# Wider query and output projections, paired modulations, shared visits for the linear attention's products and another job order in a two-layer hybrid block

## The chip, the cores and the metric

The kernel runs on one core of one Trainium2 chip. The metric is the device time in microseconds of one execution. The engines are TensorE (PE in the profile, with PEld for its weight loads), VectorE (DVE), ScalarE (ACT), GpSimd (POOL) and SyncE (SP), which here only issues DMAs.

## What is computed

Two layers of a block with three branches over 512 latent tokens (x) and 256 context tokens (c), 1024 channels, fp32 inputs. Cut to what matters here:

```python
def hybrid_layer(xs, cs, c, c_ctx, ..., need_ctx):
    shift_x, scale_x, gate_x = jnp.split(jax.nn.silu(c) @ w_mod + b_mod, 3, axis=-1)
    ...
    hx = rms_norm(xs, norm_g) * (1 + scale_x[:, None]) + shift_x[:, None]
    px = split_cols(hx @ w_in + b_in)
    ya_x = conv_module(*px[0:3], dw_w, dw_b, ln_g, ln_b, w_conv_out)      # 31 taps
    yb_x, yb_c = gla_branch(px[3:9], pc[3:9], ...)                        # both directions
    yc_x, yc_c = attn_branch(px[9:13], pc[9:13], ...)                     # softmax attention
    def merge(p, ya, yb, yc):
        return (jax.nn.sigmoid(p[13]) * ya + jax.nn.sigmoid(p[14]) * yb
                + jax.nn.sigmoid(p[15]) * yc) @ w_out
    xs = xs + gate_x[:, None] * merge(px, ya_x, yb_x, yc_x)
```

The context is updated in layer 0 only. The linear attention (`gla_branch`) has 4 heads and chunks of 64 tokens, 12 over both streams: in each chunk a state S = diag(decay) S + k^T v is carried on, in both directions, and the output is a masked product within the chunk plus q S.

## The kernel before

Every large product is made of two-part fp32r numbers: weights and activations are split in a high and a low part (`whi`, `wlo`; two tiles of `hx` for x, of `hc` for the context), and a sum over 1024 channels is 8 x 3 = 24 matrix products: high by high, low by high, high by low.

An order planner in the kernel (`Weaver`, with costs in `Engine` and the table `P`) runs the work as coroutines when the program is built, takes the ready one with the lowest priority number on each engine, and so fixes the order in which each engine's instructions stand. A recording helper makes them all, so that line 296 stands at nearly every row of the profile; groups are told apart by their tiles. The two strings `P["o0"]` and `P["o1"]` list each layer's jobs, which PE works through in turn: `q` query, key and value projections, `c` convolution inputs, `v` and `k` inputs of the linear attention, `s` and `m` gates of branches and merge, `a`, `g`, `h` modulations, and two digits for a merge job (branch, column block). Attention, linear attention, convolution and norms are further coroutines whose instructions are woven in between.

PSUM's eight banks are three pairs of tiles: `pg` and `pm`, one bank each, and `p2` (`p` in the rows), two banks each. A coroutine asks for them with `need` and gives them back with `free`. SBUF has 29 big buffers (`r3`, `r` in the rows).

The parts that the change touches:
- `TM` (line 608): a projection with tokens on the output partitions. It waits for two weight units of 4 x 256 columns, and for each token tile of 128 makes 24 products of 256 columns into one `pg` bank. `attn_jobs` (line 910) has three such jobs: keys and values for six tiles, and two halves of the query for the tiles of `qtt` (six in layer 0, four in layer 1).
- `Mod` (line 628): a column block of the modulation, with 32-column products (`r,cstat` in the rows, two records each). `mod_jobs` makes eight jobs a layer, each followed by a copy, two transposes, a reduction and six small DVE instructions; `gate_jobs` four.
- `gla_head` (line 1452): after six transposes, `states` makes the chunks' products in two blocks (8, then 6), each in one `p2` tile, and DVE carries the states on with 12 and 10 instructions of 64 x 128; `intra` makes the masked products, four to a `p2` tile, and DVE copies them under the mask (`zt`). Two heads are under way at a time.
- `OutJob` (line 1777): the output projection in four blocks of 256 columns for x and c of layer 0 and x of layer 1. It first broadcasts a piece of the gate row (`yg`) over the partitions by one product, waits for all eight pieces of the merged sum (`M`), and for each token tile makes 24 products of 256 columns into a `pg` bank; `out_ev` multiplies by the gate (`tg<-pg,gb`) and adds to the residual (`r<-r,tg`).

Of the kernel before, what the change touches and what calls it, by code (L numbers as in the profile page):

```python
# [43 lines left out]
def _consts():  # L44
# [4 lines left out]
    for v in range(2):  # L49
        for g in range(4):  # L50
# [25 lines left out]
P = dict(vb=3, pko=5, res=4, resg=0, lead=6, pbr=3, tlead=3, nf=2, nbk=4, pconv=7, mlead=2, pmain=8, lat=6,  # L76
         vm=100, am=100, gm=97)
P["o0"] = (
# [3 lines left out]
P["o1"] = (  # L82
    "c3 q0 m22 q1 q2 c0 m11 m15 c1 c6 h3 m4 m8 s11 c2 s3 s10 s5 k0 m7 s9 s2 m12 s4 s8 c5 c4 m19 c7 v1 h2 m14 "
    "v0 k1 m9 m20 k2 m16 m0 h1 s7 m21 m18 k3 m5 m23 s6 s0 s1 m17 h0 m2 m3 m10 21 22 20 23 m1 m6 m13 00 03 02 "
    "10 11 01 13 12")
# [20 lines left out]
class Weaver:  # L106
# [18 lines left out]
    def pool(self, tag, cap):  # L125
        self.avail[tag] = [0.0] * cap
# [174 lines left out]
def hybrid_kernel(ctx: ExitStack, tc: tile.TileContext, x, c, ctx_in, c_ctx, norm_g, w_mod, b_mod,  # L301
# [57 lines left out]
    gbt = mk(pr, "gb", 2)  # L359
# [4 lines left out]
    W.pool("rm", 12)  # L364
# [262 lines left out]

    class Mod:
        def __init__(self, L, cols, evac, step=4):
            self.L, self.cols, self.evac, self.step = L, cols, evac, step  # L630
            self.evs = [_Event() for _ in range(2 * len(cols))]
            self.raws = []

        def load(self):
            src = w_mod[self.L.l].rearrange("(p j) c -> p j c", j=8)
            for i in range(2 * len(self.cols)):
                yield from need(("rm", 1))
                yield from W.need_low(1)
                r = r3([4, 128])
                self.raws.append(r)  # L640
                c0 = self.cols[i // 2]
                spawn(load(self.evs[i], (r, src[:, i % 2 * 4:i % 2 * 4 + 4, c0:c0 + 128])), 0)

        def run(self):
            yield from need(("pg", 1))
            ps = pg([len(self.cols) * 128])
            n = 2 * len(self.cols)
            for i0 in range(0, n, self.step):
                yield from wait(*self.evs[i0:i0 + self.step])
                yield "+P"  # L650
                for i in range(i0, min(n, i0 + self.step)):
                    for j in range(4):
                        PE.matmul(ps[32 * j:32 * j + 32, i // 2 * 128:i // 2 * 128 + 128],
                                  lhsT=K["cstat"][:, i % 2 * 4 + j], rhs=self.raws[i][:, j],
                                  start=(i % 2 == 0), stop=(i % 2 == 1), tile_position=(0, 32 * j))
                    free("r3")
                    free("rm")
            spawn(self.evac(ps), 1)

    class Layer:  # L660
# [65 lines left out]
        def mod_jobs(S):  # L726
# [4 lines left out]
            def evac(j):  # L731
                def g(ps):
                    yield from need(("tg", 1))
                    yield "E"
                    yt = tg([256])
# [4 lines left out]
                    pt = pm([2, 128])  # L740
                    for m in range(2):
# [3 lines left out]
                    V.tensor_reduce(S.mc[:, :, j], pt.rearrange("p m (g r) -> p m r g", g=4)[:, :, 0:2, :],  # L745
                                    axis=AX.X, op=ALU.add)
# [4 lines left out]
                    for v, s in enumerate("xc"):  # L751
                        a, b = S.sh[s][:, j:j + 1], S.sc[s][:, j:j + 1]
                        V.tensor_add(a, S.mc[:, 0, j, v:v + 1], vv[:, V_BM + j:V_BM + j + 1])
                        V.scalar_tensor_tensor(b, S.mc[:, 1, j, v:v + 1], 1.0, vv[:, V_BM + 8 + j:V_BM + 9 + j],
                                               op0=ALU.add, op1=ALU.add)
                        V.tensor_mul(b, b, vv[:, V_NG + j:V_NG + j + 1])
                    fire(S.E(("mod", j)))
                return g
            return [Mod(S, [128 * j, D + 128 * j], evac(j), 1 if S.l == 0 and j < 3 else 4) for j in range(8)]

        def gate_jobs(S):
            def evac(u0):
                def g(ps):
# [3 lines left out]
                    cp(S.yg[:, u0 * 256:u0 * 256 + 256], ps)  # L767
                    free("pg")
                    S.ygn += 1
                    if S.ygn == 4:  # L770
# [4 lines left out]
            return [Mod(S, [2048 + u * 256, 2176 + u * 256], evac(u)) for u in range(4)]  # L775
# [134 lines left out]
        def attn_jobs(S):  # L910
            S.qkv = {}
            S.nq = {tt: (3 if tt in S.qtt else 1) for tt in range(6)}

            def mkev(b):
                def ev(tt, ps):
                    yield from wait(S.E("abias"))
                    if tt not in S.qkv:
                        yield from need(("r3", 1))
                        S.qkv[tt] = r3([T])
                    yield "V"  # L920
                    V.tensor_add(S.qkv[tt][:, b * 256:(b + 1) * 256], ps, S.bq[:, b * 256:(b + 1) * 256])
                    free("pg")
# [4 lines left out]
            return [TM(S, [(O_AQ + b * 256, 256)], range(6) if b == 2 else S.qtt, mkev(b)) for b in (2, 0, 1)]  # L927
# [524 lines left out]
        def gla_head(S, h):  # L1452
# [49 lines left out]
            done_s, done_a = _Event(), _Event()  # L1502

            def states():
                step = 0
                for blk, nst in (([0, 1, 2, 3, 11, 10, 4, 5], 6), ([9, 8, 7, 6, 5, 10], 5)):
                    yield from need(("p2", 1))
                    yield "P"
                    pcn = p2([2, 4, 128])
                    cnt = [0, 0]  # L1510
                    con = {}
                    for cix in blk:
                        e = cix % 2
                        r = slice(64 * e, 64 * e + 64)
                        con[cix] = pcn[:, e, cnt[e]]
                        cnt[e] += 1
                        PE.matmul(con[cix], lhsT=kt[r, cix // 2], rhs=gv[h][r, cix // 2], start=True, stop=True)
                    if step == 0:
                        nst = 6
                    for i in range(step, step + nst):  # L1520
                        for o, r in ((fo, F_), (bo, B_)):
                            yield "V" if (i == step and r == F_) else "+V"
                            V.scalar_tensor_tensor(ST(o[i + 1], r), ST(o[i], r), dec[r, o[i]:o[i] + 1], con[o[i]][r],
                                                   op0=ALU.mult, op1=ALU.add)
                    step += nst
                    free("p2")
                free("r3")
                fire(done_s)

            def intra():  # L1530
                step = 2
                for g in range(0, len(S.qtt), step):
                    tts = S.qtt[g:g + step]
                    n = len(tts)
                    yield from need(("p2", 1))
                    yield "+P"
# [189 lines left out]
        def out_ev(S, s, blk, i, ps, gb, dst, lastt):  # L1726
# [6 lines left out]
            if lastt:  # L1733
                free("gb")
# [195 lines left out]
```

## Time and profile before

| | |
|---|---|
| median of 3 runs | 1496.29 us (1494.51 to 1499.57) |
| the profiled execution's own time | 1495.49 us |
| its span in the profile | 1493.7 us |
| PE busy | 1418.5 us, 95% |
| weight loads (PEld) busy | 1239.1 us, 83% |
| DVE busy | 1149.3 us, 77% |
| ACT busy | 582.2 us, 39% |
| DMA | 187.57 MB, 126 GB/s in the mean |

The busy time of an engine is the union of its instructions; the ends of PE's products are modelled, so a busy PE may hold short waits. Tiles in the rows bear the program's names without buffer numbers, and `out<-in` tells what an instruction writes and reads; the moving operand of a product comes first, then the one that stands. A stretch of the span belongs to a stage only roughly, since the stages overlap.

### The profile page before, as it was taken

To read this page: it belongs to the slowest core of one execution; us is meant where nothing else is said; L and a number is where in the kernel's file an instruction comes from. 1 tells how busy PE (TensorE), PEld (TensorE's weight loads), DVE (VectorE), ACT (ScalarE), POOL (GpSimd) and SP (SyncE) were. 2 spreads that over 40 slices of the span, in tenths; PEclk is the share of its full clock that TensorE was granted. 3 is DMA by queue.
4 is the path that set the end of the run, shared out by engine and by line. 5 is a ranking of instruction groups with operands and counts; after the bars stand their busy time and mean duration, and the time that the engine had idled before them with its cause. 6 is when DMAs were issued, how large, how long until landed. Compare 5 with 4: busy or idle time off the path is not lost.

```text
span 1493.7 us, 24919 instructions
## 1 busy us (share of the span) xinstructions
PE 1418.5 (95%) x9520; PEld 1239.1 (83%) x9520; DVE 1149.3 (77%) x2086; ACT 582.2 (39%) x1127; POOL 248.9 (17%) x354
## 2 busy tenths in 40 slices
PE   3999999999999989998999999999999999999998
PEld 2799888888997877776888988977888988777788
DVE  4445977778987988985777574778999899998563
ACT  4423465454225232234423154344545235632320
POOL 2003312120000142100041010502322000121200
PEclk9999999999999999999999999999999999999999
DMA  9732332213232234364667354242122425455752
GB/s 271 206 111 56 93 91 84 63 35 95 80 116 74 62 92 124 104 219 150 199 195 245 112 183 121 78 134 84 50 83 80 123 78 155 117 181 173 250 170 85
DMA packets 235371, 187.57 MB, mean 126 GB/s; under 512 B 15296, under 2 KB 206322, under 8 KB 235252
## 3 DMA queue, kind: packets, MB, share of 16 engines
q1 hardware_dynamic: 234948, 185.86, 40.9%
q8 instruction: 75, 1.23, 0.3%
q14 instruction: 44, 0.36, 0.1%
q10 hardware_dynamic: 304, 0.11, 0.0%
HBM read 151.86 MB, written 34.08 MB: 124 GB/s over the span
## 4 chain that ended last, share of the span: by engine, by line
PE 62%; DVE 21%; issue 5%; POOL 4%; DMA 4%; ACT 3%; SPq 1%; ACTq 0%; DVEq 0%; POOLq 0%
PE pg L296 51%; DVE r L296 12%; PE p L296 6%; PE pm L296 4%; POOL sm L296 4%; DVE wlo L296 4%; DVE sm L296 2%; ACT r L296 1%; DVE tg L296 1%; DMA r<-ogd 1%; DVE t L296 1%; DVE whi L296 1%; SPq L314 1%; DVE zt L296 1%; DMA raw<-in_w_in 1%
## 5 line engine op out<-in xcount | busy, mean ns | idle before, releaser
L296 PE MATMUL pg<-hx,whi 128*128 128x512 f32 x1504 | 384.1, 398 | 1.1 <-ACT tg L296 0.6
L296 PEld LDWEIGHTS pg<-hx,whi 128*128 128x128 f32 x1504 | 275.4, 190 | 56.3 <-ACT tg L296 1.0
L296 DVE SCALAR_TENSOR_TENSOR r<-r,tp,r 128x768 f32<-128x768 f32 (+29 forms) x240 | 202.5, 887 | 0.4
L296 PE MATMUL pg<-hx,wlo 128*128 128x512 f32 x752 | 194.7, 393 | 0.0
L296 DVE TENSOR_TENSOR wlo<-raw,whi 128x1024 fp32r<-128x1024 f32 (+1 forms) x140 | 174.8, 1248 | 20.0 <-ACT whi L296 18.1
L296 ACT CAST whi<-raw 128x512 fp32r<-128x512 f32 (+1 forms) x194 | 115.3, 619 | 191.4 <-PE pg L296 153.6
L296 PE MATMUL pg<-whi,hx 128*128 128x256 f32 (+1 forms) x1152 | 165.4, 285 | 1.8 <-DVE hx L296 0.8
L296 PEld LDWEIGHTS pg<-hx,wlo 128*128 128x128 f32 x752 | 138.9, 188 | 28.2
L296 PEld LDWEIGHTS pg<-whi,hx 128*128 128x128 f32 x1152 | 150.0, 191 | 5.2 <-DVE tg L296 2.9
L296 ACT ACTIVATE tg<-pg,hv 128x256 f32<-128x256 f32 (+1 forms) x116 | 71.7, 618 | 211.5 <-PE pg L296 162.2
L296 DVE TENSOR_TENSOR r<-r,r 128x512 f32<-128x512 f32 (+8 forms) x208 | 123.0, 612 | 23.2 <-DMA r<-ogd 13.5
L296 PE MATMUL pg<-r,whi 128*128 128x512 f32 (+1 forms) x576 | 127.9, 363 | 7.6 <-DVE r L296 7.5
L296 POOL TENSOR_SCALAR r<-r,sm 128x768 f32<-128x768 f32 (+1 forms) x80 | 84.2, 1055 | 272.3 <-DVE sm L296 229.3
L296 PEld LDWEIGHTS pg<-r,whi 128*128 128x128 f32 x576 | 97.1, 190 | 27.1 <-DVE r L296 8.8
L296 PE MATMUL pg<-hc,whi 128*128 128x256 f32 x768 | 108.3, 290 | 4.1 <-DVE r L296 3.2
L296 PEld LDWEIGHTS pg<-hc,whi 128*128 128x128 f32 x768 | 100.6, 195 | 7.8 <-issue 3.6
L296 ACT ACTIVATE r<-p,sm 128x768 f32<-128x768 f32 (+1 forms) x80 | 65.5, 819 | 80.9 <-DVE sm L296 80.7
L296 PE MATMUL pg<-wlo,hx 128*128 128x256 f32 (+1 forms) x576 | 93.4, 284 | 0.0
L296 PE MATMUL p<-r,r 64*128 64x128 f32 (+2 forms) x672 | 90.2, 308 | 2.4 <-DVE r L296 1.1
L296 POOL TENSOR_TENSOR r<-r,r 128x512 f32<-128x512 f32 (+1 forms) x33 | 44.1, 1344 | 281.8 <-DVE r L296 251.1
L296 PE MATMUL pm<-r,r 128*128 128x256 f32 (+4 forms) x672 | 83.1, 283 | 0.9 <-DVE r L296 0.9
L296 PEld LDWEIGHTS pm<-r,r 128*128 128x128 f32 (+2 forms) x672 | 75.6, 176 | 8.4 <-DVE r L296 2.4
(151 smaller groups left out, 2056.9 us busy)
## 6 DMA issues: line engine op xcount, KB each, us to landing
raw<-in_w_in SPq DMA_DIRECT2D x116, 512.0 KB
r<-in_w_mod SPq DMA_DIRECT2D x96, 256.0 KB
thd<-tg SPq DMA_DIRECT2D x48, 256.0 KB
raw<-in_w_out SPq DMA_DIRECT2D x24, 512.0 KB
r<-thd SPq DMA_DIRECT2D x24, 384.0 KB
sgd<-tg SPq DMA_DIRECT2D x24, 256.0 KB
r<-thd SPq DMA_DIRECT2D x24, 256.0 KB
r<-sgd SPq DMA_DIRECT2D x12, 384.0 KB
```

Source lines behind the costliest of these rows:

```text
L296: return real(*a, **k)
L314: (nc.scalar if q else nc.sync).dma_start(dst, src)
```

## The change

- A class `Wide` makes a projection 512 columns wide for all token tiles at once: it takes a bank for each tile, goes through four weight units of 2 x 512 (outer loop) and all tiles (inner loop), and each tile is evacuated after the last unit.
- `QJob` is the query projection in that form (one job for two). In layer 0 its six tiles take both `p2` tiles and both `pg` banks, in layer 1 its four tiles take both `p2` tiles.
- `OutJob` is made in two blocks of 512. It begins when the first two pieces of the merged sum are there and takes the weight units in the order of the merge jobs; the gate row is broadcast before the last unit. The first block of x takes both `p2` tiles, the second both `pg` and both `pm` banks, a block of c one `p2` tile.
- `Mod` jobs are joined in twos (in layer 0: 1, 1, 2, 2, 2 column pairs; in layer 1 four times 2; gates two a layer), with weights loaded in thirds of 3, 3 and 2 rows.
- In `gla_head` one coroutine makes a block of state products and a group of inner products in one visit of PE, and takes a `p2` tile for each at once.
- The job strings and some of the planner's costs and priorities are new.

```diff
-P = dict(vb=3, pko=5, res=4, resg=0, lead=6, pbr=3, tlead=3, nf=2, nbk=4, pconv=7, mlead=2, pmain=8, lat=6,
-         vm=100, am=100, gm=97)
+P = dict(vb=3, pko=12, res=4, resg=0, lead=6, pbr=2, tlead=3, nf=2, nbk=3, pconv=6, mlead=2, pmain=6, lat=6,
+         vm=100, am=100, gm=101)
-    "a3 a2 m19 k3 q2 q1 m2 q0 s11 s4 c3 m5 m3 m9 c4 s3 m22 a4 c1 g0 k1 c0 c2 m0 m16 s1 k0 v0 m7 m23 s5 v1 m21 "
+    "m4 q0 q1 s7 m15 c3 m16 s6 m13 m2 s2 c0 c1 c2 k0 m8 m1 m21 c4 k3 v0 g1 m11 m18 m20 v1 s11 k1 c6 m10 c7 c5 "
...
+    class Wide:
+        def __init__(self, src, col0, order=range(4)):
+            self.order = list(order)
+            self.us = [Unit(src, 256 * i, 2, [(col0, 512)]) for i in self.order]
...
+        def mm(self, tiles, ps, ready, evac, mid=None):
+            for q, (i, u) in enumerate(zip(self.order, self.us)):
+                yield from wait(u.ev)
+                if mid is not None and q == 3:
+                    yield from mid()
+                for t, (h, rows) in enumerate(tiles):
+                    yield from ready(i, t)
+                    w, hl = u.w, h
+                    yield from gemm(ps[t][0], tm_terms(w, hl, rows, 2 * i), start=q == 0, stop=q == 3)
+                    if q == 3:
+                        spawn(evac(t, *ps[t]), 1)
+                free("whi")
+                free("wlo")
...
+            ps = yield from self.banks(len(tts), (("p2", 2), ("pg", 2)))
...
     class Mod:
+        ROWS = ((0, 3), (3, 6), (6, 8))
...
+        def load1(self, ev, r, src, j0, j1, c0, c1):
+            if c1 == c0 + 128:
+                dma(r[:, :j1 - j0].rearrange("p j m c -> p j (m c)"), src[:, j0:j1, c0:c0 + 256])
+            else:
+                for m, c in enumerate((c0, c1)):
+                    dma(r[:, :j1 - j0, m], src[:, j0:j1, c:c + 128])
...
-            return [TM(S, [(O_AQ + b * 256, 256)], range(6) if b == 2 else S.qtt, mkev(b)) for b in (2, 0, 1)]
+            return [TM(S, [(O_AQ + 512, 256)], range(6), mkev(512, 768)), QJob(S, mkev(0, 512))]
...
+            def products():
+                for b in range(max(len(groups), 2)):
+                    yield from need(("p2", (b < 2) + (b < len(groups))))
+                    yield "P" if b == 0 else "+P"
+                    if b < 2:
+                        pcn = p2([2, 4, 128])
...
+                            PE.matmul(con[cix], lhsT=kt[r, cix // 2], rhs=gv[h][r, cix // 2], start=True, stop=True)
+                    if b < len(groups):
+                        tts = groups[b]
+                        pa = p2([2, 4, 128])[:, :, 0:len(tts)]
...
-            if blk == 0:
-                yield from wait(*[S.E(("M", s, m)) for m in range(8)])
...
+            yield from wait(S.E(("M", s, 2 * self.order[0])))
+            ps = yield from self.banks(n, (("p2", 2),) if blk == 0 or n < 4 else (("pg", 2), ("pm", 2)))
...
+            def ready(i, t):
+                yield from wait(*[S.E(("M", s, 2 * i + k)) for k in range(2)])
```

Three places of the instructions' order, before and after. The first is PE in layer 0's output projection of x; `pg` or `p` is the sum of a token tile (a `p` tile holds two), `whi` and `wlo` the parts of a weight unit. Before, at the end of the first tile's sum:

```order
L296 MATMUL pg_8633<-whi_8486,hx_8177 128x256
L296 MATMUL pg_8633<-whi_8486,hx_8178 128x256
L296 MATMUL pg_8633<-wlo_8487,hx_8177 128x256 x4
L296 MATMUL pg_8670<-whi_8401,hx_8177 128x256
L296 MATMUL pg_8670<-whi_8401,hx_8178 128x256
```

After, at the end of the third weight unit:

```order
L296 MATMUL p_1304_8407<-whi_8412,hx_8068 128x512
L296 MATMUL p_1304_8407<-wlo_8413,hx_8067 128x512 x2
L296 MATMUL pm_8505<-yg_4236,cst 128x512
L296 MATMUL p_1303_8406<-whi_8446,hx_8067 128x512
L296 MATMUL p_1303_8406<-whi_8446,hx_8068 128x512
```

A tile's sum was finished before the next began; now the weight unit changes only after all tiles, and the broadcast of the gate row stands between the third unit and the fourth.

The second is PE at the linear attention of layer 0; `p` with `r,r` are its products (four of a group of inner products, six or eight of a block of states), the `pg` rows are gate jobs. Before:

```order
L296 MATMUL p_906_5654<-r_850_5227,r_872_5392 128x128 x4
L296 MATMUL pg_5607<-hx_342,wlo_5406 128x512 x3
L296 MATMUL p_907_5666<-r_849_5226,r_864_5332 128x128 x4
L296 MATMUL p_908_5672<-r_739_4234,r_862_5330 128x128 x6
L296 MATMUL pg_5607<-hx_342,wlo_5406 128x512 x3
L296 MATMUL p_910_5687<-r_849_5226,r_864_5332 128x128 x4
```

After, the first visit:

```order
L296 MATMUL pg_5675<-hc_271,wlo_5473 128x256 x8
L296 MATMUL p_896_5727<-r_678_3847,r_870_5579 128x128 x8
L296 MATMUL p_897_5736<-r_856_5429,r_872_5581 128x128 x4
L296 MATMUL pg_5726<-hx_329,whi_5472 128x512
```

States and inner products came in visits of their own or together, as the planner found room; now a block of states and a group of inner products always come together, and the next block of the same head comes only after the first block of another.

The third is DVE in layer 1's softmax attention; `sm<-p` is the maximum of a block of scores, a row with `tp` a convolution tap, `t<-pm` takes the attention's output from PSUM, `r<-p` the transposed probabilities. Before, from the tenth to the twelfth of the 32 maxima:

```order
L296 TENSOR_REDUCE sm_11122<-p_1768_11082 128x1
L296 SCALAR_TENSOR_TENSOR r_1653_10508<-r_1622_10305,tp_7407,r_1653_10508 128x502
L296 SCALAR_TENSOR_TENSOR r_1730_10896<-r_1718_10851,tp_7407,r_1730_10896 128x502
L296 RECIPROCAL sm_11122<-sm_11122 128x1
L296 SCALAR_TENSOR_TENSOR r_1653_10508<-r_1622_10305,tp_7407,r_1653_10508 128x503
L296 TENSOR_TENSOR t_1776_11146<-pm_11124,t_1776_11146 64x256
L296 TENSOR_REDUCE sm_11161<-p_1774_11140 128x1
L296 TENSOR_REDUCE sm_11167<-p_1777_11151 128x1
```

After, from the tenth to the eleventh:

```order
L296 TENSOR_REDUCE sm_10408<-p_1673_10385 128x1
L296 RECIPROCAL sm_10402<-sm_10402 128x1
L296 RECIPROCAL sm_10408<-sm_10408 128x1
L296 CAST r_1669_10380<-p_1678_10420 128x3x128
L296 TENSOR_TENSOR r_1670_10381<-p_1678_10420,r_1668_10379 128x3x128
L296 TENSOR_TENSOR r_1671_10382<-p_1678_10420,r_1669_10380 128x3x128
L296 TENSOR_REDUCE sm_10445<-p_1679_10428 128x1
```

The taps that stood between the maxima are gone from this place; they stand further on.

## Rows read from the trace of the kernel before

**Rows 1.** Part 1 of the page: busy us, share of the span, instructions.
```profile
PE 1418.5 (95%) x9520; PEld 1239.1 (83%) x9520; DVE 1149.3 (77%) x2086; ACT 582.2 (39%) x1127; POOL 248.9 (17%) x354
```

**Rows 2.** Stretches: from:to, length, busy us of each engine, clock, DMA, GB/s.
```profile
165.70:344.60 178.90, 175.62 (x1205) 156.21 (x1204) 137.51 (x289) 94.31 (x220) 44.92 (x61) 1.00 0.24 69
...
506.10:598.10 92.00, 83.65 (x702) 69.87 (x701) 82.81 (x162) 25.10 (x46) 28.44 (x54) 0.96 0.34 98
...
999.80:1148.20 148.40, 141.80 (x810) 119.92 (x809) 136.68 (x238) 77.34 (x164) 42.20 (x31) 0.99 0.26 74
1148.20:1281.00 132.80, 131.52 (x819) 113.91 (x817) 122.12 (x193) 59.77 (x101) 7.66 (x8) 1.00 0.40 113
```

**Rows 3.** Timeline of PE, output projection: start us, us, what, count.
```profile
841.09 0.59 PE L296 MATMUL pg<-yg,cst 128*128 128x256 f32 x2
841.77 1.22 PE L296 MATMUL pg<-whi,hx 128*128 128x256 f32 x8
...
843.31 1.12 PE L296 MATMUL pg<-whi,hx 128*128 128x256 f32 x8
...
844.75 1.12 PE L296 MATMUL pg<-whi,hx 128*128 128x256 f32 x8
```

**Rows 4.** Timeline of PE, a gate job with 512 tokens.
```profile
730.41 3.82 PE L296 MATMUL pg<-hx,whi 128*128 128x512 f32 x16
734.07 1.98 PE L296 MATMUL pg<-hx,wlo 128*128 128x512 f32 x8
735.88 2.08 PE L296 MATMUL pg<-hc,whi 128*128 128x256 f32 x16
```

**Rows 5.** Timeline of PE, modulation visits at the start.
```profile
43.68 1.95 PE L296 MATMUL pg<-r,cstat 128*32 128x128 f32 x64
45.56 0.44 PE L296 MATMUL pm<-cst,tg 128*128 128x128 f32 x2
45.93 1.08 PE L296 MATMUL pg<-r,cstat 128*32 128x128 f32 x32
46.94 1.00 PE L296 MATMUL pm<-cst,tg 128*128 128x128 f32 x4
```

**Rows 6.** Timeline of PE, an fp32 product of 512 columns.
```profile
714.47 1.02 PE L296 MATMUL pm<-r,cst 128*128 128x512 f32 x2
714.93 1.16 PE L296 MATMUL pg<-r,whi 128*128 128x256 f32 x5
```

**Rows 7.** Timeline of PE, two visits of the linear attention.
```profile
522.38 1.61 PE L296 MATMUL p<-r,r 64*128 64x128 f32 x24
...
557.31 0.71 PE L296 MATMUL p<-r,r 64*128 64x128 f32 x8
```

**Rows 8.** DVE in layer 1's attention: taps (busy us, mean ns), maxima (ns, first to last start).
```profile
L296 DVE SCALAR_TENSOR_TENSOR r<-r,tp,r 128x497 f32<-128x497 f32 (+14 forms) x60 | 44.0, 753 | 0.1
...
L296 DVE TENSOR_REDUCE sm<-p x32: 926/942/959, 999.8 to 1148.2; 128x1 f32<-128x768 f32 x32
```

**Rows 9.** DVE: the last instruction of the timeline; the nearest 512-wide group (busy us, mean ns).
```profile
1490.27 0.42 DVE L296 TENSOR_TENSOR r<-r,tg 128x256 f32<-128x256 f32 x1
...
L296 DVE SCALAR_TENSOR_TENSOR r<-r,pg 128x512 f32<-128x512 f32 x48 | 32.7, 684 | 24.6 <-PE pg L296 22.6 <-issue 1.9
```

**Rows 10.** Timeline of SP's DMA issues at the start: start us, us, what, count.
```profile
12.30 10.74 SPq L314 DMA_DIRECT2D r<-in_w_mod  x12
23.09 2.26 SPq L314 DMA_DIRECT2D raw<-in_w_in  x2
```

**Rows 11.** Timeline of PE, an output job of the context; in brackets the wait before it.
```profile
874.84 1.22 PE L296 MATMUL pg<-whi,hc 128*128 128x256 f32 x8 [2.02 <-DVE tg L296]
```

**Rows 12.** Waits of DVE, 450 to 715 us: us in total, times, longest.
```profile
DVE zt L296 <- PE p L296: 1.5, 2, 1.0
DVE r L296 <- PE p L296: 1.3, 2, 0.8
```

More of the change, by code (lines that the diff above doesn't have):

```diff
@@ L363, in hybrid_kernel @@
     W.pool("aP", 4)
-    W.pool("rm", 12)
+    W.pool("rm", 9)
     pg = mk(pp, "pg", 2)
@@ L626, in run, with banks, done @@
             free("wlo")
-    class Mod:
-        def __init__(self, L, cols, evac, step=4):
-            self.L, self.cols, self.evac, self.step = L, cols, evac, step
-            self.evs = [_Event() for _ in range(2 * len(cols))]
+    class Wide:
+        def __init__(self, src, col0, order=range(4)):
+            self.order = list(order)
+            self.us = [Unit(src, 256 * i, 2, [(col0, 512)]) for i in self.order]
+        def banks(self, n, tags):
+            took, left = [], n
+            for t, k in tags:
+                m = 2 if t == "p2" else 1
+                while k and left > 0:
+                    took.append((t, min(m, left)))
+                    left -= m
+                    k -= 1
+            yield from need(*[(t, sum(x == t for x, _ in took)) for t in dict(took)])
+            ps = []
+            for t, m in took:
+                hold = [m]
+                b = {"p2": p2, "pg": pg, "pm": pm}[t]([m, 512])
+                def done(hold=hold, t=t):
+                    hold[0] -= 1
+                    if hold[0] == 0:
+                        free(t)
+                ps += [(b[:, i], done) for i in range(m)]
+            return ps
+        def mm(self, tiles, ps, ready, evac, mid=None):
[11 more added lines that the diff above has]
+                free("wlo")
@@ L1501, in gla_head @@
             bo = list(range(NCC - 1, -1, -1)) + list(range(NCH - 1, NCC - 1, -1))
[L1502 to L1528, printed above, removed]
@@ L1551, in gla_head, with states @@
-            spawn(intra(), 3)
-            spawn(states(), 3)
-            yield from wait(done_s, done_a)
+            done_a = _Event()
+            blks = ([0, 1, 2, 3, 11, 10, 4, 5], [9, 8, 7, 6, 5, 10])
+            groups = [S.qtt[g:g + 2] for g in range(0, len(S.qtt), 2)]
+            chain = [_Event(), _Event()]
+            def states(b, pcn, con, i0, i1):
+                if b:
+                    yield from wait(chain[0])
+                for i in range(i0, i1):
+                    for o, r in ((fo, F_), (bo, B_)):
+                        yield "V" if (i == i0 and r == F_) else "+V"
+                        V.scalar_tensor_tensor(ST(o[i + 1], r), ST(o[i], r), dec[r, o[i]:o[i] + 1], con[o[i]][r],
+                                               op0=ALU.mult, op1=ALU.add)
+                free("p2")
+                fire(chain[b])
@@ L1554, in gla_head @@
+            spawn(products(), 3)
+            yield from wait(*chain, done_a)
             left = [len(qs)]
@@ L1784, in run @@
             if blk == 0:
[L1785 removed]
+                for i in range(n):
                     spawn(S.x_load(s, i), 4)
[L1787 to L1796 removed]
@@ L1810, in run, with ready @@
+            def ready(i, t):
+                yield from wait(*[S.E(("M", s, 2 * i + k)) for k in range(2)])
+            tiles = [(S.M[s], slice(i * 128, i * 128 + 128)) for i in range(n)]
+            yield from self.mm(tiles, ps, ready, lambda t, b, done: S.out_ev(s, blk, t, b, done, self), gate)
+            if blk == 1:
                 free("hx" if s == "x" else "hc", 2)
```

255 lines of the change are left out of this document (145 added, 110 removed), and 2 rows, old and new, of the table vm.

## The prediction

> **What bounds the kernel now.** I read the busy times first. TensorE (PE) is busy 95% of the span and VectorE (DVE) 77% [rows 1]: a microsecond taken out of the PE stream should come out of the span unless DVE holds the PE there. Three stretches say where DVE does [rows 2]. From 506.1 to 598.1 us (first to last step of the state chains of layer 0's linear attention) DVE works 82.8 of 92.0 us and PE stands idle 92.0 - 83.65 = 8.35. From 999.8 to 1148.2, the softmax attention of layer 1, DVE works 136.7 of 148.4 us and PE is idle 6.6. From there to the state chains of layer 1, at 1281.0, DVE works 122.1 of 132.8 us, but PE is idle only 1.3. Elsewhere PE is the limit: in layer 0's softmax attention, 165.7 to 344.6, DVE works 137.5 of 178.9 us and PE is idle 3.3.
>
> The sum is made against the profiled execution, 1495.5 us (span 1493.7 and 1.8 around it); the median of the three runs shown is 0.8 above it.
>
> **The change, part by part.**
>
> *512 columns instead of 256.* The query projection has 6 + 4 token tiles over two blocks of 256 columns, the output projection 4 + 2 + 4 tiles over four blocks, at 24 products each: 10 x 2 x 24 + 10 x 4 x 24 = 1440 products of 256 columns become 720 of 512. In a stretch with nothing else 12 products of 256 columns take 844.75 - 843.31 = 1.44 us, 120 ns each [rows 3]. 24 products of 512 columns take 735.88 - 730.41 = 5.47 us, 228 ns each [rows 4]. Each block of 24 wide products thus saves 48 x 0.120 - 5.47 = 0.29 us, and 30 blocks save **8.6 us**, all in stretches where PE is the limit. In rows 4 the operands change places (the weights stand, the tokens move), but shape and type are the same, so I take 228 ns. The bounds are small: at 240 ns nothing is gained; below 228 no row goes.
>
> The Trainium skill, "TensorE: Matmul & The Clock Gate", section "Back-to-back issue gap", gives about 131 ns for a 512-column product in a sustained stream. By that page 720 x (240 - 131) ns = 78 us would go, an estimate from its figure. The rows show 228 ns for this shape, so the measurement decides and the page's figure gets no chance.
>
> *Modulations in twos.* The 24 modulation jobs stand in 22 separate visits before and in 14 after. A visit of 64 records takes 45.56 - 43.68 = 1.88 us, one of 32 takes 46.94 - 45.93 = 1.01 [rows 5], so joining two saves 0.14 us, 8 times: **1.1 us**. The small DVE instructions that go, and the gate rows' new place in the big buffers, lie beside a busy PE; I count them at nothing.
>
> *Gate rows.* 12 broadcasts of 256 columns become 6 of 512. One takes 841.77 - 841.09 = 0.68 us [rows 3], which is 0.24 of streaming at 120 ns a record and 0.44 besides. Two records of 512 columns in the same type stream in 714.93 - 714.47 = 0.46 us [rows 6]. With the same 0.44 that is 0.90, and 12 x 0.68 - 6 x 0.90 = **2.8 us** goes. Bounds: 0 if the 0.44 doubles too, 5.4 if it vanishes.
>
> *Linear attention's products.* 192 products in 24 visits become 192 in 20. Visits of 24 and of 8 records take 1.61 and 0.71 us [rows 7]: 0.056 a record and 0.26 a visit. Four visits fewer save **1.0 us**. What it costs that one visit takes both wide PSUM tiles is a rival below.
>
> *The job order, layer 0.* The diff does not tell what moves, the order of instructions does. Between the first and the last visit of layer 0's linear attention PE has 132 products of 256 columns and 129 of 512 from other jobs before, 132 x 0.120 + 129 x 0.228 = 45 us, and 264 and 273 after, 94 us: the merge of the attention branch and more gate jobs now stand there. PE then has something to do while DVE works through the chains. The nearest stretch in which DVE and PE share work with enough at hand is layer 0's softmax attention, where PE idles 3.3 of 178.9 us [rows 2]; at that share 92 us would leave 1.7, and **6.6 us** of the 8.35 close. Bounds: nothing, since the merges bring DVE work of their own, and 8.35.
>
> *The job order, layer 1.* Of the convolution taps 60 stand on DVE between the first and the last softmax maximum before, and 31 after. A tap costs 44.0 / 60 = 0.73 us there [rows 8], so 29 x 0.73 = 21 us leave that stretch and enter the next. The first gives back at most PE's idle 6.6 us. The next has 132.8 - 122.1 = 10.7 us of DVE free, so up to 21 - 10.7 = 10.5 us may lengthen it. I take the two as even, 0, with -6.6 and +10.5 as the ends. In layer 0 the 43 taps that were hidden under the merge now stand ahead of the last state step; they move with PE work, and I count them at nothing. If that cover fails, the linear attention starts late.
>
> *The end.* The last tile is evacuated 512 wide: two DVE instructions of 0.68 us, as the nearest row of that width from PSUM, instead of two of 0.42 [rows 9]: **0.5 us** more.
>
> *The loads.* Layer 0's modulations come in 48 issues instead of 32, each of 192 or 128 KB instead of 256. 12 issues took 10.74 us, 0.895 each, but two of 512 KB took 2.26, 1.13 each [rows 10]: time goes more with bytes than with issues. I take nothing, with 16 x 0.895 = 14.3 us as the upper bound, if each issue keeps its price.
>
> *Sum.* 8.6 + 1.1 + 2.8 + 1.0 = 13.5 us less PE work, 6.6 less waiting, 0.5 more at the end: 1495.5 - 19.6 = **1476 us**. With the ends of the order's two terms and of the gate rows, which won't all fall on one side, this case runs from about 1466 to 1486.
>
> **The rivals.**
>
> *The wide jobs wait for banks.* The layer-0 query job takes six of the eight PSUM banks at once and gives its results all in its last quarter; the output jobs take four. Each of the eight wide jobs (five in layer 0, three in layer 1) then has an edge at which PE waits for an evacuation. The trace has one such edge at an output job: PE waited 2.02 us for DVE [rows 11]. Eight of them cost 16 us and leave 1476 + 16 = **1492 us**, about no change. Against it: the last quarter works tile by tile, 6 x 0.228 = 1.4 us apart, and an evacuation of 0.7 us fits between. The Trainium skill, "Perfetto Trace Analysis", section "Optimizing Tensor Performance", says that independent products should rotate through PSUM banks so that evacuation overlaps the next group's products, which speaks against holding them; by that rule the edges stay. Rows 11 agree with it, for one edge.
>
> *The linear attention's DVE runs dry (slower).* A visit now needs both wide PSUM tiles free, so a head's next visit starts only when its chain of states and its masked copy are done, and its next chain only after that visit. A head has two such edges in layer 0 and one in layer 1: 12. Each costs a visit (0.26 + 20 x 0.056 = 1.4 us) and up to 1.0 us until DVE goes on, the longest such wait [rows 12]: 2.4 us, 29 in all, and **1505 us**. It decides if at least 9 of the 12 edges are bare (11 for more than 0.3% slower); each one filled by the other head, by taps or by splits is free. Against it: around that stretch DVE waited for these products four times, 2.8 us together, before [rows 12], and in the new order the other head's chain often stands between. For it: DVE is 90% busy there [rows 2], so what it loses PE loses.
>
> *The start issues by count.* The loads' upper bound: 1476 + 14 = **1490 us**. The small price per byte of the 512 KB loads speaks against it.
>
> *The new order moves nothing that matters.* Then only the PE work goes: 1495.5 - 13.0 = 1482.5 us, inside the forecast's range.
>
> **How the numbers follow.** Forecast, 1466 to 1486: 0.56. More waiting closes, below 1466: 0.08. Waits for banks: 0.16. Issues by count: 0.06. DVE runs dry: 0.14. The range has to reach to the waits for banks and part of the way to the slower case: **1462 to 1499**; that leaves about 0.05 below and 0.13 above. 0.3%, about what a measurement of this kernel can tell from no change, is 4.5 us, so faster means under 1491.8 and slower over 1500.8. Faster: 0.56 + 0.08, half of the banks' case and most of the issues': 0.75. Same: the rest of those two and part of the slower case: 0.12. Slower: 0.13.
>
> **What would show it.** Right, step by step: products of the form 128x512 from hx or hc in the query and output jobs start 228 ns apart; 14 modulation visits; PE busy falls by about 13 us; PE idle between the first and last state step of layer 0 falls from 8.35 to some 2 us; in layer 1 the time from the first softmax maximum [rows 8] to the first state step stays within -7 and +10 us of 281. Wrong: wide products at 240 ns; PE waits of 2 us at the edges of the query or output jobs; DVE idle behind PE's products between the linear attention's chains; layer 0's first products starting later.

## The result, and the profile after

The changed kernel takes 1475.6 us (median of 4 runs, 1475.07 to 1477.53) where the kernel before took 1497.9 on the same chip (1494.51 to 1502.07): a ratio of 0.9852, 95% interval 0.9823 to 0.9881. A second set of runs, on another chip, gave 1474.44 us and 0.9852 again (0.9828 to 0.9876). The forecast was 1476.

First the changed kernel's page, part 1 (busy us, share of the span, instructions), which answers [rows 1].

```profile
PE 1406.2 (95%) x8788; PEld 1198.3 (81%) x8788; DVE 1140.2 (77%) x2009; ACT 575.6 (39%) x1095; POOL 249.8 (17%) x354
```

PE's busy time fell by 1418.5 - 1406.2 = 12.3 us; the span fell by 18.0, from 1493.7 to 1475.7. The other 5.7 us are PE's idle time, 75.2 before and 69.5 after. Where it lies is told by the stretches between the same events in both kernels: first and last softmax maximum of a layer, first step of its state chains, last merge product. Of the changed kernel (from:to, length, busy us of each engine, granted clock, DMA share, GB/s):

```profile
0.00:167.00 167.00, 136.62 (x953) 115.82 (x954) 83.05 (x202) 59.43 (x122) 32.97 (x69) 0.99 0.49 140
167.00:340.40 173.40, 169.63 (x1107) 148.89 (x1105) 132.44 (x271) 93.82 (x214) 36.44 (x49) 1.00 0.23 62
340.40:543.60 203.20, 202.91 (x1432) 182.79 (x1432) 184.65 (x252) 69.40 (x120) 1.47 (x5) 1.00 0.40 112
543.60:681.10 137.50, 128.88 (x931) 108.74 (x930) 118.77 (x235) 48.03 (x80) 37.12 (x58) 0.99 0.45 142
681.10:804.60 123.50, 121.97 (x819) 105.14 (x818) 86.94 (x141) 40.84 (x69) 28.42 (x30) 1.00 0.63 205
804.60:995.30 190.70, 183.28 (x894) 150.74 (x893) 129.82 (x231) 68.38 (x134) 30.70 (x60) 1.00 0.43 129
995.30:1127.60 132.30, 129.04 (x763) 110.00 (x762) 115.22 (x211) 71.02 (x152) 37.34 (x31) 1.00 0.26 73
1127.60:1268.40 140.80, 135.95 (x821) 118.05 (x820) 137.04 (x217) 59.24 (x101) 10.07 (x7) 0.98 0.40 113
1268.40:1422.30 153.90, 150.66 (x881) 120.74 (x880) 128.82 (x227) 58.90 (x94) 35.24 (x46) 1.00 0.57 186
```

Of the kernel before, the stretches that [rows 2] don't have (506.1 to 813.2 is layer 0's linear attention and merge in one):

```profile
0.00:165.70 165.70, 141.81 (x1179) 124.46 (x1180) 82.94 (x213) 60.94 (x125) 26.05 (x59) 0.98 0.55 157
344.60:506.10 161.50, 157.99 (x1030) 143.56 (x1029) 140.77 (x202) 55.09 (x96) 1.89 (x6) 0.98 0.31 89
...
506.10:813.20 307.10, 286.58 (x1905) 244.37 (x1904) 249.86 (x429) 99.20 (x170) 61.92 (x88) 0.98 0.49 157
```

Length less PE busy is PE's idle time. In layer 0's linear attention and merge it fell from 307.1 - 286.6 = 20.5 us to 8.6 + 1.5 = 10.1: the largest gain, 10.4 us. Ahead of that, from the last maximum to the first state step, it fell from 3.5 to 0.3. But the start, up to the first maximum, lost: 165.7 - 141.8 = 23.9 us idle became 30.4. In layer 1 the attention gained (6.6 to 3.3) what the next stretch lost (1.3 to 4.8). So a good part of what the total shows is a difference of gains and losses that the total hides. The busy time is no pure measure of work either: kernels with the same 8788 products, in other orders, keep PE busy between 1399.9 us (experiment 5, single modulations, mean granted clock 0.997) and 1415.3 (experiment 4, 0.981).

### The profile page after: what moved, and what is told of

Read it like the earlier page. It is cut to its first block, busy times and chain, and to the rows that moved or that the text cites. A ratio compares the mean times of both kernels' runs of the same rounds, so it can differ in the third digit from the quotient of the medians.

```text
span 1475.7 us, 23372 instructions
## 1 busy us (share of the span) xinstructions
PE 1406.2 (95%) x8788; PEld 1198.3 (81%) x8788; DVE 1140.2 (77%) x2009; ACT 575.6 (39%) x1095; POOL 249.8 (17%) x354
## 5 line engine op out<-in xcount | busy, mean ns | idle before, releaser
L296 DVE TENSOR_TENSOR wlo<-raw,whi 128x1024 fp32r<-128x1024 f32 (+1 forms) x140 | 171.3, 1224 | 17.3 <-ACT whi L296 16.5
L296 ACT CAST whi<-raw 128x512 fp32r<-128x512 f32 (+1 forms) x184 | 109.1, 619 | 192.3 <-PE pg L296 101.1
L296 DVE TENSOR_TENSOR r<-r,r 128x512 f32<-128x512 f32 (+7 forms) x208 | 120.8, 605 | 13.3 <-ACT r L296 5.3
L296 POOL TENSOR_SCALAR r<-r,sm 128x768 f32<-128x768 f32 (+1 forms) x80 | 77.2, 967 | 278.1 <-DVE sm L296 240.5
L296 DVE CAST whi<-raw 128x512 fp32r<-128x512 f32 (+1 forms) x96 | 42.1, 440 | 60.1 <-PE pg L296 22.8
L296 DVE TENSOR_TENSOR r<-p,r 128x384 fp32r<-128x384 f32 (+2 forms) x152 | 77.6, 543 | 14.0 <-ACT r L296 9.2
L296 POOL TENSOR_TENSOR r<-r,r 128x512 f32<-128x512 f32 (+1 forms) x33 | 48.5, 1474 | 234.2 <-DVE r L296 106.4
L296 PEld LDWEIGHTS p<-r,r 64*128 64x128 f32 (+1 forms) x672 | 68.8, 188 | 18.8 <-issue 6.3
L296 PE MATMUL pg<-whi,hx 128*128 128x272 f32 (+2 forms) x480 | 82.2, 309 | 0.0
```

The costliest lines, as they stand in the source:

```text
L296: return real(*a, **k)
```

## The experiments

Each kernel ran 4 to 12 times, beside the kernel before. Differences are told against the changed kernel by its own time on the same chip where it ran there (1474.44 us), else by the two ratios to the kernel before.

**1. The width alone.** The planner is charged as before for one wide product, so no instruction changes its place; only the product itself is issued as two.

```diff
+            half = k.pop("half", False)
...
+            if half:
+                for o in (0, 256):
+                    real(a[0][:, o:o + 256], lhsT=k["lhsT"], rhs=k["rhs"][:, o:o + 256],
+                         start=k["start"] and o == 0, stop=k["stop"] and o == 256)
+                return
             return real(*a, **k)
```

> The changed kernel with nothing moved: the same order on every engine, but each of the 720 products 512 columns wide of the query and output jobs is issued as two products of 256 columns into the halves of the same bank. Theory A (the saving is fixed TensorE work: 228 ns for one wide product against 2 x 120 ns, and all of it lies on the path): slower than the changed kernel by 720 x 0.012 = 8.6 us, so 1484 us, TensorE busy up by 7 to 10 us. Rival B (what the wide products save is waited away again at the edges of the wide jobs, where the banks' readers are late): 0 to 3 us, 1476 to 1479 us, TensorE's idle time down by as much as its busy time is up. Rival C (the width is worth more than its products' time, since narrow ones also pull their weight loads into the open): over 12 us, above 1488 us.

Measured: 1479.94 us, ratio 0.9888 (0.9867 to 0.9908). Against the changed kernel's ratio, from another chip, that is some 4 to 5 us with an interval as large, so the same kernel ran again beside the changed one:

> The changed kernel itself, unchanged, as the yardstick on this chip for the three that follow. All theories: 1473.5 to 1478 us.

> The changed kernel with each wide product issued as two of 256 columns, nothing moved, this time beside the changed kernel on one chip: the first comparison went over two chips and gave 4.3 us, half of 720 x 0.012 = 8.6 us. Theory A (all of the wide products' saving lies on the path): 7 to 10 us above the unchanged one. Theory B (half of it is covered by waits on the weights at the edges of the wide jobs): 3 to 6 us. Rival C (nothing is left of it): 0 to 2 us.

Measured: 1474.44 us for the changed kernel (1473.05 to 1476.69) and 1479.91 for the narrow one (1478.45 to 1481.01; ratio 0.9889, 0.9867 to 0.9911): 5.5 us. The products do what the rows promised. PE's timeline in layer 0's output job for the context, unchanged and then narrow (start us, us, what, count):

```profile
852.23 1.07 PE L296 MATMUL p<-whi,hc 128*128 128x512 f32 x4
...
853.59 1.07 PE L296 MATMUL p<-whi,hc 128*128 128x512 f32 x4
```

```profile
857.09 1.12 PE L299 MATMUL p<-whi,hc 128*128 128x256 f32 x8
858.05 0.64 PE L299 MATMUL p<-wlo,hc 128*128 128x256 f32 x4
858.53 1.12 PE L299 MATMUL p<-whi,hc 128*128 128x256 f32 x8
```

Six wide products take 853.59 - 852.23 = 1.36 us, 227 ns each; twelve narrow ones take 1.44, 120 ns each. PE's busy time is 1412.9 us narrow and 1404.9 unchanged, 8.0 apart. But its idle time is 1479.2 - 1412.9 = 66.3 us narrow and 70.0 unchanged. Of 8 us of work, then, some 3 filled waits that are there anyhow. Theory B holds in size: about two thirds of the saving reached the end. That the waits are for weights is not shown; the ones that are shorter in the narrow kernel are mostly for DVE and ACT. Between the first state step of layer 0 and the first softmax maximum of layer 1, for instance, the wide products save 4.8 us of PE's busy time (439.1 and 434.3), but the stretch is only 2.8 us shorter (454.6 and 451.8).

**2. The order.** The new jobs in the old order with the old planner's numbers, and the old jobs in the new:

```diff
-P = dict(vb=3, pko=12, res=4, ...
+P = dict(vb=3, pko=5, res=4, ...
-    "m4 q0 q1 s7 m15 c3 ...
+P["o0"] = "a1 m19 k3 q0 q1 m2 ...
```

> The changed kernel's jobs (wide products, modulations in twos, shared visits), run in the job order and with the planner's numbers of the kernel before, translated: the query job stands where the first of the two narrow ones stood, a modulation of two where the later one of its two stood. Theory A (13.5 us of fixed TensorE work less, some 6 us by the order): 1482 to 1487 us. Rival B (the order does nearly all of it, the wider products little): 1490 to 1497 us. Rival C (the order has no part in it): 1473 to 1479 us.

> The kernel before (256 columns, single modulations, separate visits) in the new job order and with the planner's new numbers, translated: where the order names the query job of 512 columns the two narrow ones stand, where it names a modulation of two the two single ones stand. Theory A (the order alone gives 6 us of TensorE's idle time in layer 0): 1489 to 1492 us. Rival B (the order does nearly all): 1474 to 1482 us. Rival C (an order fits one set of jobs alone, and this one was made for the wide ones): no faster than the kernel before, 1495 to 1510 us.

Measured: 1499.95 us (ratio 1.0014, 0.9999 to 1.0029) and 1500.07 (1.0018, 1.0004 to 1.0032). Both are as slow as the kernel before, and all three theories on the first are wrong: the new jobs in this order bring nothing. PE is busy 1409.3 us there, 9.2 less than before, but idles 90.5, 15.3 more; 7.5 of them lie ahead of the first softmax maximum (31.3 for 23.9), where the joined modulations are (experiment 5). The second is as its rival C has it. Neither has more than a small part of the gain in layer 0. Its linear attention and merge, in the first and in the second:

```profile
510.60:821.40 310.80, 291.48 (x1943) 249.19 (x1940) 252.33 (x414) 97.56 (x164) 64.19 (x88) 0.97 0.51 162
```

```profile
536.70:813.20 276.50, 259.02 (x1757) 218.18 (x1757) 203.54 (x396) 90.17 (x154) 61.21 (x88) 0.97 0.51 163
```

PE idles 19.3 and 17.5 us there, where the kernel before idles 20.5 and the changed kernel 10.1.

**3. The shared visits.** In the changed kernel, state products and inner products apart again, each with its own wide PSUM tile; then the reverse, the shared visits alone put into the kernel before:

```diff
-            def products():
-                for b in range(max(len(groups), 2)):
-                    yield from need(("p2", (b < 2) + (b < len(groups))))
...
-            spawn(products(), 3)
-            yield from wait(*chain, done_a)
+            spawn(intra(), 3)
+            spawn(states(), 3)
+            yield from wait(done_s, done_a)
```

> The changed kernel with linear attention's state products and inner products in visits of their own, as in the kernel before (24 visits of TensorE where 20 stand), all else as it is. Theory A (a visit costs 0.2 us and no more): 0.5 to 2 us slower than the changed kernel. Rival B (the shared visits are what shortened layer 0's linear attention and merge by 16 us of TensorE waits, which neither the old order with the new jobs nor the new order with the old jobs has): 6 to 16 us slower. Rival C (the earlier hold of two banks costs): 1 to 4 us faster.

> The kernel before with one part of the change alone: state products and inner products of linear attention in shared visits, in its own job order. Theory A (a shared visit saves 0.2 us four times, the rest of the 14.7 us that undoing it in the changed kernel costs belongs to the order): within 5 us of the kernel before, on either side. Rival B (holding two banks for a shared visit spaces the heads out, so that other products cover them, whatever the order): 8 to 16 us faster than the kernel before.

Measured: apart, 1489.1 us (ratio 0.9947, 0.9928 to 0.9966), 14.7 above the changed kernel. Alone in the kernel before, 1494.08 against 1496.56 (0.9986, 0.9969 to 1.0002): 2.5 us or nothing. The visits have no such price of their own; layer 0's stretches with the visits apart show where it lies, the chains and then the rest up to the last merge product:

```profile
544.20:645.90 101.70, 93.06 (x721) 77.61 (x722) 92.77 (x174) 29.07 (x50) 32.41 (x56) 0.97 0.45 142
645.90:816.10 170.20, 161.42 (x1027) 138.36 (x1026) 110.76 (x201) 59.56 (x98) 29.21 (x32) 0.99 0.55 178
```

The same jobs in the same list, but the chains end after 101.7 us instead of 137.5, with DVE busy 92.8 of them, and the merge that stood between them now comes behind. PE idles 17.4 us instead of 10.1, and the whole lasts 271.9 us instead of 261.0. With two wide tiles to a visit the heads start later, and the merge's products stand between them; whether the tiles or the planner's other decisions do that was not separated.

**4. One number of the planner.**

```diff
-         vm=100, am=100, gm=101)
+P = dict(vb=3, pko=12, ... vm=100, am=100, gm=97)
```

> The changed kernel with one number of the planner set back: it charges GpSimd's operations at 97 hundredths of its cost rule, as in the kernel before, instead of 101. No instruction and no operand changes, only the order that the planner writes. Theory A (the order is fitted to its planner's numbers to the last per cent, so that the 14.7 us of the separate visits and the 25 us of the translated orders are in good part the price of any order that was not looked for): 10 to 30 us slower than the changed kernel, 1485 to 1505 us, with the layer 0 stretch from the first state step to the last merge product longer than 261 us. Rival B (the order is robust, and those prices are those of the parts): within 4 us of the changed kernel.

Measured: 1512.09 us, ratio 1.0109 (1.0088 to 1.0130): about 38 us above the changed kernel and 16 above the kernel before, more than any part of the change is worth. Theory A holds, and beyond its range; its place was wrong, since layer 0's stretch is 261.3 us long as before. The largest loss is in layer 1, where convolution taps come late. DVE's taps between the first state step and the last merge product (count, busy us, mean ns):

```profile
L289 DVE SCALAR_TENSOR_TENSOR r<-r,tp,r 128x510 f32<-128x510 f32 (+14 forms) x29 | 22.9, 830 | 0.0
```

All engines in that stretch:

```profile
1271.90:1456.60 184.70, 158.65 (x882) 125.08 (x881) 156.88 (x262) 59.66 (x97) 38.10 (x49) 0.93 0.48 156
```

PE's timeline in it, in brackets the wait ahead:

```profile
1401.03 0.80 PE L289 MATMUL pg<-r,whi 128*128 128x512 f32 x1 [8.86 <-ACT r L289]
1405.74 3.23 PE L289 MATMUL pg<-r,whi 128*128 128x512 f32 x7 [3.92 <-DVE r L289]
1408.81 1.08 PE L289 MATMUL pg<-r,wlo 128*128 128x512 f32 x4
1409.73 2.02 PE L289 MATMUL pg<-r,whi 128*128 128x512 f32 x8
```

In the changed kernel this stretch has no tap, DVE works 128.8 of 153.9 us and PE idles 3.2. Here DVE works 156.9 us, and the 29 taps are 22.9 of the 28 us more. PE idles 184.7 - 158.7 = 26 us; its longest waits, of 8.9 and 3.9 us, are for the inputs (`r`) of the merge's products, and with a granted clock of 0.93 the same products also take 8 us more. The last of the taps ends at 1356.4 us; that the waits from 1392 us on follow from the taps is read from the order and was not tested by itself.

**5. The modulations of layer 0 single again** (the number of jobs whose loads start at once goes with it), and then four single and two of two:

```diff
-            for n in ((1, 1, 2, 2, 2) if S.l == 0 else (2, 2, 2, 2)):
+            for n in ((1,) * 8 if S.l == 0 else (2, 2, 2, 2)):
...
-                if cur[0] < i - P["mlead"] and i >= 5:
+                if cur[0] < i - P["mlead"] and i >= 8:
```

> The changed kernel with the eight modulations of layer 0 singly again (those of layer 1 and the gates stay in twos and fours), so the first columns of the norm come earlier: between the start and the first attention step the changed kernel loses about 9 us more to TensorE waits than the kernel before, two of them of 5 us before the first shift and scale columns. Theory A (the columns by twos cause that): 3 to 6 us faster than the changed kernel, 1470 to 1473 us, with three more visits costing 0.4 us. Rival B (the start waits for its bytes, however they are grouped): within 1.5 us of the changed kernel. Rival C (the single visits keep a bank and delay the first products): 2 to 5 us slower.

> The changed kernel with layer 0's modulations as four single ones and then two of two (two single ones and three of two in the changed kernel, eight single ones in the run that was 8.7 us faster). Theory A (the first columns are what the start waits for): all or nearly all of the gain, 1466 to 1469 us. Theory B (each of two delays its own columns, and the later ones count as well): about a third of it, 1471 to 1474 us. Rival C (the gain was the order's luck): above 1475 us.

Measured: single, 1466.93 us, ratio 0.9799 (0.9777 to 0.9821), 0.53% or some 8 us below the changed kernel; four single, 1469.19, ratio 0.9831 (0.9807 to 0.9855), 3 to 5 us below it. Theory A of the first holds, beyond its range: the joined visits are a loss. The result of the second lies between the ranges of its theories A and B. The gain of the first is there by the first softmax maximum, which comes at 157.3 us with single modulations and at 165.9 in the changed kernel's second profile. With four single it comes at 158.3, so the first columns carry nearly all of what the start gains, as theory A has it; the rest of the difference arises later. The stretch from 33 to 42 us in that profile, then two joined visits on its PE, then the same stretch with single modulations:

```profile
33.00:42.00 9.00, 6.57 (x73) 5.10 (x74) 3.75 (x6) 3.26 (x7) 0.00 (x0) 0.62 1.09 287
```

```profile
37.46 3.64 PE L296 MATMUL pg<-r,cstat 128*32 128x128 f32 x64
...
49.52 1.96 PE L296 MATMUL pg<-r,cstat 128*32 128x128 f32 x64
```

```profile
33.00:42.00 9.00, 8.45 (x108) 6.28 (x110) 6.58 (x26) 5.99 (x12) 0.00 (x0) 1.00 1.04 280
```

With joined visits PE idles 2.4 of the 9 us, its granted clock is 0.62, and a visit of 64 records takes 3.64 us, near twice the 1.96 of the next one: it ran at the lower of the two levels. With single ones PE idles 0.6, the clock is 1.00, and 108 products are done instead of 73. DVE and ACT do nearly twice the work, which fits the norm's columns coming one by one. Over the whole way to the first maximum PE has 954 records in both kernels; all engines, with joined and with single visits:

```profile
0.00:165.90 165.90, 135.72 (x954) 115.19 (x954) 83.05 (x202) 59.28 (x122) 32.67 (x69) 0.97 0.49 141
```

```profile
0.00:157.30 157.30, 131.53 (x954) 111.33 (x954) 86.86 (x225) 57.73 (x120) 32.66 (x69) 1.00 0.51 149
```

Of the 8.6 us, 4.4 are waits (30.2 and 25.8 us idle) and 4.2 are slower products. That price was measured in the new order alone: the kernel before, with single modulations, also has a low clock from 33 to 42 us, and reaches its first maximum at 165.7, with more products ahead of it:

```profile
33.00:42.00 9.00, 7.53 (x27) 6.28 (x28) 3.15 (x5) 2.54 (x6) 0.00 (x0) 0.62 1.09 305
```

**6. Layer 1's order of the kernel before**, layer 0's new one kept:

```diff
-    "m13 q1 s10 m19 q0 m11 ...
+P["o1"] = "c3 q1 m22 q0 c0 m11 ...
```

> The changed kernel with layer 1's job order of the kernel before (translated), layer 0's new order and the planner's new numbers kept. Theory A (layer 1's new order brought the 8 us that lie between its first softmax maximum and its first state step): 6 to 10 us slower than the changed kernel, with that stretch back at 281 us. Rival B (those 8 us come from the wide query job and the planner's numbers): within 3 us of the changed kernel, the stretch at 273 us. Rival C (the new order of layer 1 does harm): 3 to 8 us faster.

Measured: 1470.83 us, ratio 0.9824 (0.9799 to 0.9850), 3.6 below the changed kernel: the new order of layer 1 does harm. From first maximum to first state step the stretch is 269.4 us where the changed kernel has 273.1 and the kernel before 281.2, so those 8 us did not come from layer 1's order. PE's idle time in it is 4.7, 8.4 and 7.9 us. PE's timeline of the changed kernel (second profile) shows what the new order adds, and below it stand all engines around that place:

```profile
1224.15 6.45 PE L296 MATMUL pg<-hx,whi 128*128 128x512 f32 x16 [4.11 <-DVE yg L296]
```

```profile
1219.00:1232.00 13.00, 8.89 (x59) 7.04 (x52) 12.93 (x15) 5.04 (x6) 2.82 (x1) 0.74 0.36 98
```

PE waited 4.1 us for DVE, busy 12.9 of the 13 us, to copy a joined gate modulation (`yg`) out of the bank that the next job wants, and the 16 products behind the wait took 6.45 us where 16 take 3.82 [rows 4]. With the old order ACT makes this copy too, as it does the other three in both kernels, and PE waits 0.7 us for it. Behind this stretch the old order waits 1.8 us more (11.5 for 9.7), so not all of that gain reaches the end.

**7. Both harms undone**, single modulations and layer 1's old order in the changed kernel:

> The changed kernel with both parts undone that did harm: layer 0's eight modulations single, and layer 1's job order that of the kernel before (translated). Theory A (they lie in different stages, so the gains of 7.5 to 8.7 and of 3.6 us add up): 1462 to 1465 us, and 2.1 to 2.5 per cent below the kernel before. Rival B (the second gain is eaten where the first moved the start of layer 1): 1466 to 1470 us.

Measured: 1464.44 us (1463.72 to 1466.15), ratio 0.9792 (0.9771 to 0.9813). It is the fastest of all, 2.1% below the kernel before; but the second gain shrank from 3.6 us to between 1 (by the ratios) and 2.5 (by the times). The time lies in theory A's range and below rival B's, but the shrunken second gain is what B describes, and the intervals don't tell whether the two gains add up.

## Why the prediction was right, and where its steps were not

The time, the sign and the kind of cause came as forecast: less PE work (12.3 us busy, forecast 13.5) and less waiting (5.7, forecast 6.6). Under the sum its steps did less well, and their errors cancelled. That the time came within 1 us of the forecast is luck: from layer 0's last softmax maximum to its last merge product PE waits 13.6 us less, twice what the sum has, and ahead of the first maximum 6.5 more, which no step has. And of the 22 us between the two kernels only the width's 5.5 are shown with the order held. How the rest divides between the new jobs and the new order stays open: each without the other brought nothing (experiment 2).

- **512 columns, 8.6 us.** The pace was right, 227 ns for 228, and by PE's busy time the size too (8.0). The step that failed is that all 30 blocks lie where PE is the limit: 5.5 us reached the end. The Trainium skill's 131 ns ("TensorE: Matmul & The Clock Gate", "Back-to-back issue gap") are not seen in these products; the measurement decides.
- **Modulations in twos, 1.1 us.** The sign was wrong: in the new order they cost some 8 us. The step counted visits and put what hangs on them "at nothing". It didn't ask who waits for the first columns at the start, where PE idles 30.2 of 165.9 us, and where the products were slower as well (mean granted clock 0.97, with single visits 1.00).
- **Gate rows, 2.8 us.** Not tried by itself. In the new order of layer 1 a joined gate modulation brought a wait of 4.1 us that the step didn't have; in the old order the wait behind the joined visit is 0.7 (experiment 6).
- **Shared visits, 1.0 us.** Alone in the kernel before they gave 2.5 us or nothing, in line with it. In the changed kernel taking them out cost 14.7, with all that the planner then ordered otherwise.
- **Layer 0's order, 6.6 us.** The gain is there and larger, 10.4 us, but not where the step put it. Between the first and last state step PE still idles 8.6 us (8.35 before), now in 137.5 us with the merge's products in between. The merge behind the chains had idled 20.5 - 8.35 = 12.2 us, and it idles 1.5 now. Nor is it the order alone: with the old order or the old jobs most of it is lost, with separate visits 7.3 us.
- **Layer 1's order, 0.** By PE's waits, which the step weighed, it was right: 6.6 + 1.3 = 7.9 us before, 3.3 + 4.8 = 8.1 after. The stretch is 8.1 us shorter, just past the forecast's end of -7, because 8.3 us less of PE's work lies in it (273.3 and 265.0). With the old order PE waits 3.7 us less there.
- **The loads, 0.** Right: SP issued 12 loads of 192 KB and 6 of 128 KB in 10.65 us, where 12 of 256 KB took 10.74 [rows 10]. The bytes are the same, 3072 KB, and so is the time, with half as many issues again.
- **The end, 0.5.** Right in size: the last DVE instructions take 0.69 us each, as taken, and from the last merge product to the end PE idles 6.1 us, 5.5 before; that stretch holds other waits too.

Of the rivals, that wide jobs wait for banks is real but small, and it lies elsewhere than at the jobs' edges. PE's waits in the changed kernel (us, times, longest); then one of them in the timeline of the second profile; then DVE's waits from 450 to 715 us there:

```profile
PE p L296 <- DVE tg L296: 6.4, 6, 2.3
```

```profile
862.65 0.86 PE L296 MATMUL p<-whi,hc 128*128 128x512 f32 x3
...
865.03 0.68 DVE L296 TENSOR_TENSOR tg<-p,r 128x512 f32<-128x512 f32 x1
...
865.77 0.51 PE L296 MATMUL p<-whi,hc 128*128 128x512 f32 x1 [2.26 <-DVE tg L296]
```

```profile
DVE r L296 <- PE p L296: 0.4, 1, 0.4
DVE zt L296 <- PE p L296: 0.2, 1, 0.2
```

Six waits of the output jobs add up to 6.4 us and two of the query jobs to 1.8, not 16. All eight stand inside the sum of the second of two token tiles that share a two-bank `p` tile, after three of the last unit's six products: PE goes on only when DVE has read the first one's half, here at 865.71 us. The output blocks whose sums have one-bank tiles (`pg`, `pm`) have no such wait; there the trace agrees with the Trainium skill's rule ("Perfetto Trace Analysis", "Optimizing Tensor Performance") that independent products should rotate through banks, so that one is evacuated during the next. Whether single tiles would save the 8 us was not tried. That linear attention's DVE runs dry is refuted: it waits 0.6 us for the products there, 2.8 before [rows 12]. And "the new order moves nothing that matters" had its opposite: the order can move more (38 us, experiment 4) than all the work that was taken out (13.5).

## What to carry to other kernels

Where a planner writes the order, part of any change's effect is the new order: before crediting a part, change one number of the planner that moves no work, and see how far the time swings (here 38 us, against 5.5 for the best-founded saving). To price a part, keep the order fixed and change only what is issued, as in experiment 1. Joining visits saves little (2.5 us or nothing in experiment 3) and costs where the first result is awaited, so look at the start and at the buffers apart from the rest.

## What the runs showed of the hardware

After some waits PE's products ran at half pace for a while, so that a wait cost more than its length. After 4.1 us of idling the next 16 products took 6.45 us instead of 3.82, 2.6 us on top, and the granted clock of the 13 us around them is 0.74. Behind two waits of 8.9 and 3.9 us (experiment 4) seven products took 3.23 us, 0.46 each, and the next eight 2.02, 0.25 each. At the start, with PE idle 2.4 of 9 us in waits of at most 1.6, the granted clock was 0.62, between the levels of 1.2 and 2.4 GHz. The first profile of the same kernel has the same visit of 3.64 us with 1.00 in that stretch's clock, so the pace of the products is the surer sign. Behind a wait of 2.3 us in an output job (865.77 us in the changed kernel's second profile) the products kept their pace. The mean granted clock of the span is lower where the kernel is slower: 0.981 in the kernel of experiment 4, 0.989 before, 0.995 after (0.993 in its second profile), 0.997 with single modulations.
